# Moving a scan's chunk systems into the order in which the scan reads them: two ways of storing them

## The chip, the core and the metric

The kernel runs on one core of a Trainium2 chip, in one launch. The metric is the device time of one execution in microseconds; a lower number is better. The core has a matrix engine (TensorE, PE in the profile, with its weight loads listed as PEld), a vector engine (VectorE, DVE), a scalar engine (ScalarE, ACT), GpSimd (POOL) and SyncE (SP), which in this kernel only issues transfers. The sixteen DMA engines of the core carry out what SP's queue and ACT's queue issue.

## The reference, cut to what matters

The layer has an attention branch and a gated DeltaNet branch that scans the 256 context and 256 latent positions of 8 heads in both directions, in chunks of 64 positions. For each chunk the scan needs the solution of a unit lower triangular system of 64 by 64:

```python
m = jnp.where(strict, jnp.einsum('bhnid,bhnjd->bhnij', kb, k) * decay, 0.0)
rhs = jnp.concatenate([v * beta, kb * jnp.exp(gc)[..., None]], axis=-1)
sol = lax.linalg.triangular_solve(m + jnp.eye(c, dtype=m.dtype), rhs,
                                  left_side=True, lower=True, unit_diagonal=True)
u, w = sol[..., :dv], sol[..., dv:]
...
def step(s, inp):
    u_c, w_c, k_c, g_c = inp[:4]
    v_new = u_c - jnp.einsum('bhcd,bhde->bhce', w_c, s)
    s_next = s * g_c + jnp.einsum('bhcd,bhce->bhde', k_c, v_new)
```

There are 8 heads, 8 chunks and 2 directions, so 128 systems. The kernel does not solve them one by one: it inverts all 128 matrices at once and multiplies by the inverse inside the scan.

## The kernel before, in words

The program is a chain of stages. Weights are read in float32 in tiles of 128 by 1024 (`raw`, a ring of 8 buffers), split into a rounded part `whi` (ACT, L123) and a remainder `wlo` (DVE, L124), and multiplied with activations that are split in the same way. A second user of the ring are the tiles `rawa` of the modulation matrix, which DVE reduces beside all stages.

1. **First projection** (to about 145 us). The activations `xl` and `xc` arrive in eight transfers of 512 KB, their squares are summed on PE (`pss`), and for each of 16 slices of the model dimension the modulation columns (`wt`, `raw<-in_wadab`) and the first weights (`gr<-in_wfirst`) are used as soon as they land (`amp`, `fp`).
2. **The heads' stage** (to about 390 us). For each head, the rest of the input projection and `dn_head`, which among other things makes the strictly triangular matrix `U` of each chunk. `U` is stored to DRAM as blocks of 32 by 32: the two diagonal blocks to `Ud`, the off-diagonal one to `Uo`.
3. **The inverse** (`inverse`, L822, run in pieces beside the key and value projections, to about 480 us). All 128 systems lie on the 128 partitions of `ux`: partition 32 g + 16 d + s holds system (g, d, s), where d is the direction, g is a head modulo 4 and s counts chunk and half of the heads. DVE inverts both diagonal blocks. The result is stored twice: as `Xq` for the off-diagonal product (8 stores, L846), and into `Tt` by 16 stores (L851), one for each g, d and diagonal block b. Each of them moves 512 runs of 128 bytes.
4. **The latent attention** (to about 700 us). Beside the attention's matmuls and the gate projections (`gtp`), `off_diagonal` (L854) makes the off-diagonal blocks in 8 rounds q: it loads `uo` and `xd`, multiplies twice with block-diagonal matrices (`ivp`) and stores the product to `Tt` with 4 transfers a round (L892, 128 runs of 128 bytes each).
5. **The scan** (from about 720 us) reads `Tt`, one piece for each chunk (`tt<-Tt`, L1273). `Tt[64 d + 32 b + c, s, g, 32 e + j]` is row 32 b + c, column 32 e + j of the inverse. The block that is always zero (rows of b = 1, columns below 32) is stored once, from a tile of zeros, `none`, by two transfers of 2048 runs of 128 bytes (L656).
6. Branch projections, output projection and the gated feed-forward layer fill the rest.

What sets the order: PE's instructions are kept in the order in which the program is written (`pe.pinned`) for nearly all of it. The other engines and the two queues are ordered by a scheduler that places an instruction where it believes its inputs to be ready. `osync` is SP with its order kept. A generator such as `off_diagonal` runs as a `Side`: it is called with an allowance, and each `yield` says how much of it was used up.

Two rules of the built program matter below. The completion of a transfer is signalled on one of eight semaphores, `DMAHW0` to `DMAHW7`, which SP's and ACT's transfers share in rotation; a transfer that is given a semaphore waits until the transfer that had it before has landed. And a tile that is laid where another tile was waits for the last reader of the old one: the pool `pc2` of the attention, in which the small tile `km` of `k_norm` (L1035) lies, reuses the space of `ux`.

Of the kernel before, what the change touches and what calls it, by code (L numbers as in the profile page):

```python
# [8 lines left out]
F32 = mybir.dt.float32  # L9
# [44 lines left out]
def hybrid_block(ctx: ExitStack, tc: tile.TileContext, io, dbg=None):  # L54
    nc = tc.nc
    act, dve, pool, sync = nc.scalar, nc.vector, nc.gpsimd, nc.sync
# [19 lines left out]
    osync = Ordered(nc.sync)  # L76
# [3 lines left out]
    def pool_(name, bufs, side="left"):  # L80
        return tc.tile_pool(name=name, bufs=bufs, side=side, reuse_waits="tile")
# [8 lines left out]
    dram = ctx.enter_context(tc.tile_pool(name="dram", bufs=1, space=DRAM))  # L90
# [10 lines left out]
    none = const.tile([P, 32], F32, name="none")  # L101
# [154 lines left out]
    def ada_rest():  # L256


        def load(i):
            w = wr.tile([P, GR], F32, tag="raw", name="rawa", bufs=NR)  # L260
            c, n = divmod(i, 32)
            sync.dma_start(w, io["wada2"][c, (n // 16 + c) % 2, n % 16])
            return w

        parts = ad.tile([P, 2, 16], F32, name="parts")
        half, ahead = None, [load(0), load(1)]
        for i in range(128):
            c, n = divmod(i, 32)
            h, j = (n // 16 + c) % 2, n % 16
            if h != half:  # L270

                for _ in range(1 if i else 0):
                    yield 1300
                half, sch = h, ad.tile([P, GR], F32, tag="sch", name="sch")
                sync.dma_start(sch, Sc[h])
                for _ in range(3):
                    yield 1300
            w = ahead.pop(0)
            if i < 126:
                ahead.append(load(i + 2))  # L280
            (odve if ada.bound else dve).tensor_tensor_reduce(out=w, in0=w, in1=sch, scale=1.0, scalar=0.0, op0=ALU.mult, op1=ALU.add, accum_out=parts[:, h, j : j + 1])  # L281
            if n == 31:
                cs = slice(16 * c, 16 * c + 16)
                dve.tensor_tensor(out=adaT[:, cs], in0=parts[:, 0], in1=parts[:, 1], op=ALU.add)
                dve.tensor_tensor(out=adaT[:, cs], in0=adaT[:, cs], in1=bada[:, 32 + 16 * c : 48 + 16 * c], op=ALU.add)
                ada.done = c + 1
            yield 1300
# [240 lines left out]
    for j in range(2 * N1):  # L528
        dst = dkx[:, j].rearrange("p a b -> p (a b)")
# [59 lines left out]
    g = pg.tile([P, 8, 8], F32, name="gx")  # L589
# [60 lines left out]
    Ud = dram.tile([4, 32, 2, 32, 32], F32, name="Ud")  # L650
    Uo = dram.tile([4, 32, 32, 32], F32, name="Uo")

    Xq = dram.tile([2, 32, 4, 32, 32], F32, name="Xq")
    Tt = dram.tile([P, 16, 4, 64], F32, name="Tt")
    for d in range(2):
        act.dma_start(Tt[64 * d + 32 : 64 * d + 64, :, :, 0:32].rearrange("c s g j -> c (s g) j"), none[:32].unsqueeze(1).broadcast_to([32, 64, 32]))  # L656
    As = dram.tile([4, P, 8, 64], F32, name="As")
    conv = mid.tile([P, 24, 3], F32, name="conv")
    dve.tensor_scalar(out=conv, in0=off["dn_conv"].rearrange("p (f w) -> p f w", w=3), scalar1=0.5, scalar2=None, op0=ALU.mult)
# [114 lines left out]
    def head_inputs(h, side=lambda c: None):  # L774
# [12 lines left out]
        gather(ps, P, xq[:, 0])  # L787
        return xs[0], xs[1], xq

    ada = Side(ada_rest())  # L790
    ada.done, ada.bound = 0, True
    ins = {h: head_inputs(h) for h in (3, 0)}
# [29 lines left out]
    def inverse():  # L822


        pI = ExitStack()
        pi = pI.enter_context(pool_("pi", 1, "right"))
        ux = pi.tile([P, 2560], F32, name="ux")
        flat = ux[:, 0:2048]
        X = flat.rearrange("p (b c j) -> p b c j", b=2, j=32)
        tmp = ux[:, 2048:]  # L830
        sync.dma_start(flat, Ud.rearrange("g r b j i -> (g r) (b j i)"))
        yield 0
        for j in range(1, 31):
            m = 31 - j
            t = tmp[:, : 2 * j * m].rearrange("p (b c i) -> p b c i", b=2, i=m)
            dve.tensor_tensor(out=t, in0=X[:, :, 0:j, j].unsqueeze(3).broadcast_to([P, 2, j, m]),
                              in1=X[:, :, j, j + 1 :].unsqueeze(2).broadcast_to([P, 2, j, m]), op=ALU.mult)
            dve.tensor_tensor(out=X[:, :, 0:j, j + 1 :], in0=X[:, :, 0:j, j + 1 :], in1=t, op=ALU.add)
            yield 150 + 4.2 * j * m
        dve.memset(flat.rearrange("p (b x) -> p b x", b=2)[:, :, 0:1024:33], 1.0)  # L840
        xt = pi.tile([P, 32, 32], F32, name="xt")
        act.copy(xt, X[:, 0].rearrange("p c j -> p j c"))
        for g in range(4):
            gs = slice(32 * g, 32 * g + 32)
            for n, x in enumerate((xt, X[:, 1])):
                sync.dma_start(Xq[n, :, g], x[gs])  # L846
        for g in range(4):
            for d in range(2):
                for b in range(2):
                    rs = slice(64 * d + 32 * b, 64 * d + 32 * b + 32)  # L850
                    sync.dma_start(Tt[rs, :, g, 32 * b : 32 * b + 32].rearrange("c s j -> s c j"), X[32 * g + 16 * d : 32 * g + 16 * d + 16, b])  # L851
        yield 1000
        pI.close()

    def off_diagonal():

        pI = ExitStack()
        pi = pI.enter_context(pool_("pj", 1, "right"))
        bd = [pi.tile([P, 4, P], F32, name=f"bd{n}") for n in range(2)]
        for n in range(2):  # L860
            pool.memset(bd[n], 0.0)

        def load(q):
            rs = slice(4 * q, 4 * q + 4)
            uo = pi.tile([P, 4, 32], F32, tag="uo", name="uo", bufs=2)
            sync.dma_start(uo, Uo[:, :, rs].rearrange("g j r i -> (g j) r i"))
            xd = pi.tile([P, 2, 4, 32], F32, tag="xd", name="xd", bufs=2)
            for n in range(2):
                sync.dma_start(xd[:, n], Xq[n, rs].rearrange("r g j c -> (g j) r c"))
            return uo, xd  # L870

        ahead = load(0)
        yield OD
        for q in range(8):
            uo, xd = ahead
            if q < 7:
                ahead = load(q + 1)
            for n in range(2):
                src = uo if n == 0 else ip
                for g in range(4):  # L880
                    gs = slice(32 * g, 32 * g + 32)
                    act.copy(bd[n][gs, :, gs], src[gs])
                yield OC / 2
                ip = psa.tile([P, 4, 32], F32, tag="aux", name="ivp")
                for r in range(4):
                    pe.matmul(ip[:, r], bd[n][:, r], xd[:, n, r], start=True, stop=True)
                if n == 0:
                    yield OC / 2
            act.copy(uo, ip)
            for g in range(4):  # L890
                dst = Tt[64 * (q // 4) : 64 * (q // 4) + 32, 4 * (q % 4) : 4 * (q % 4) + 4, g, 32:64]
                sync.dma_start(dst, uo[32 * g : 32 * g + 32])  # L892
            yield OC / 2
        pI.close()

    Ys = dram.tile([P, HEADS, T], F32, name="Ys")
# [44 lines left out]
    pn = pN.enter_context(pool_("pn", 1))  # L941
    pn2 = pN.enter_context(pool_("pn2", 2))
    inv = Side(inverse())
    inv(1)
    bq = pn.tile([P, 1, T], F32, name="bq")
# [43 lines left out]
    pN.close()  # L989
    pc2 = pC.enter_context(pool_("pc2", 2))  # L990
    inv = Side(off_diagonal())

    def mm3(ps, a, b, first, last):
# [206 lines left out]
    for b in range(4):  # L1200
# [4 lines left out]
        for n in range(7):  # L1205
            for st in (pr, tail, at):
                c = next(st, None)
# [286 lines left out]
    for f in range(NFF):  # L1494
        xs = []
        for w in ("wgate", "wval"):
# [6 lines left out]
            x = pf2.tile([P, T], F32, tag=w, name="fx")  # L1503
# [13 lines left out]
    for f in range(KD):  # L1517
# [8 lines left out]
        src = ps[:, :T]  # L1526
        if f < KD - 1:
            gather(ps, P, yx)
            src = yx
# [105 lines left out]
```

## Time and profile before

| | |
|---|---|
| median of 3 runs | 1783.9 us (1779.87 to 1786.72) |
| the profiled execution | 1786.89 us, span of its instructions 1785.1 us |
| PE busy in the span | 1737.5 us (97%) |
| DVE, ACT, POOL busy | 1356.8, 950.5, 41.4 us |
| DMA | 190,260 packets, 417.15 MB, 56,912 packets under 512 bytes |
| matmul clock granted, mean | 0.985 of full speed |

The page's row of tenths cuts the span into 40 slices of 44.6 us; a digit is the busy share of an engine in that slice, 9 standing for 90% or more. `PEclk` is the granted matmul clock in tenths. In a view of windows, each row gives the busy time of an engine in a stretch, and at its end the granted clock, the share of the time in which the sixteen DMA engines were busy, and the GB/s that they moved. In a view of waits, a row reads: engine and line that waited, what ended the wait, total us, number of times, longest. In a timeline, a row starts with the time at which a run of equal instructions started and its length in us; SPq and ACTq are issues of transfers.

### The profile page before, as it was taken

To read this page: it belongs to the slowest core of one execution; us is meant where nothing else is said; L and a number is where in the kernel's file an instruction comes from. 1 tells how busy PE (TensorE), PEld (TensorE's weight loads), DVE (VectorE), ACT (ScalarE), POOL (GpSimd) and SP (SyncE) were. 2 spreads that over 40 slices of the span, in tenths; PEclk is the share of its full clock that TensorE was granted. 3 is DMA by queue.
4 is the path that set the end of the run, shared out by engine and by line. 5 is a ranking of instruction groups with operands and counts; after the bars stand their busy time and mean duration, and the time that the engine had idled before them with its cause. 6 is when DMAs were issued, how large, how long until landed. Compare 5 with 4: busy or idle time off the path is not lost.

```text
span 1785.1 us, 34155 instructions
## 1 busy us (share of the span) xinstructions
PE 1737.5 (97%) x12957; PEld 1507.2 (84%) x12957; DVE 1356.8 (76%) x2696; ACT 950.5 (53%) x1966; POOL 41.4 (2%) x48
## 2 busy tenths in 40 slices
PE   7999999999799999999999999999999999999999
PEld 5887888888688888788878888888888888888888
DVE  4677799879578879787779979887788887655554
ACT  3335454454477766665646546555555555544443
POOL 0000011000000000000010000000000000000000
PEclk8999999999899999999989999999999999999999
DMA  9992588783578868999647968776667776666662
GB/s 348 407 373 93 150 235 249 230 257 109 138 255 248 260 214 273 360 339 361 233 130 233 328 199 281 232 237 207 202 219 229 228 225 201 182 198 199 198 199 87
DMA packets 190260, 417.15 MB, mean 234 GB/s; under 512 B 56912, under 2 KB 95696, under 8 KB 187792
## 3 DMA queue, kind: packets, MB, share of 16 engines
q1 hardware_dynamic: 165024, 401.59, 68.7%
q10 hardware_dynamic: 25072, 13.39, 2.5%
q8 instruction: 101, 1.65, 0.4%
q14 instruction: 63, 0.52, 0.1%
HBM read 387.00 MB, written 27.79 MB: 232 GB/s over the span
## 4 chain that ended last, share of the span: by engine, by line
PE 63%; issue 8%; DMA 1%; DVE 1%; ACT 0%; SPq 0%; POOL 0%; POOLq 0%; DVEq 0%
PE fps L68 27%; PE dps L68 13%; PE gtp L68 11%; PE brp L68 3%; PE vps L68 1%; PE kps L68 1%; PE qps L68 1%; PE sps L68 1%; PE kp L68 1%; PE ivp L68 1%; PE op L68 1%; PE yps L68 1%; PE yp L68 0%; DMA YM<-Ys 0%; SPq L851 0%
## 5 line engine op out<-in xcount | busy, mean ns | idle before, releaser
L123 ACT CAST whi<-raw 128x512 fp32r<-128x512 f32 (+1 forms) x940 | 578.9, 620 | 413.6 <-PE dps L68 113.5
L124 DVE TENSOR_TENSOR wlo<-raw,whi 128x512 fp32r<-128x512 f32 (+1 forms) x940 | 637.3, 686 | 211.4 <-ACT whi L123 203.5
L68 PE MATMUL fps<-H,whi 128*128 128x512 f32 x1376 | 475.0, 394 | 3.1 <-DVE H L1472 3.1
L68 PE MATMUL fps<-H,wlo 128*128 128x256 f32 x1376 | 372.3, 280 | 0.0
L68 PEld LDWEIGHTS fps<-H,whi 128*128 128x128 f32 x1376 | 253.7, 189 | 54.7 <-issue 1.9
L68 PEld LDWEIGHTS fps<-H,wlo 128*128 128x128 f32 x1376 | 259.7, 189 | 7.5 <-DVE wlo L124 0.5
L68 PE MATMUL gtp<-h,whi 128*128 128x512 f32 x640 | 231.4, 399 | 0.0
L68 PE MATMUL mmp<-h,whi 128*128 128x512 f32 x640 | 229.5, 400 | 0.0
L68 PE MATMUL dps<-GB,whi 128*128 128x512 f32 (+1 forms) x595 | 195.7, 377 | 0.0
L68 PE MATMUL mmp<-h,wlo 128*128 128x256 f32 x640 | 177.5, 283 | 0.0
L68 PE MATMUL gtp<-h,wlo 128*128 128x256 f32 x640 | 173.9, 282 | 0.0
L68 PE MATMUL dps<-GB,wlo 128*128 128x256 f32 x560 | 155.2, 282 | 0.0
L68 PEld LDWEIGHTS gtp<-h,whi 128*128 128x128 f32 x640 | 120.5, 190 | 25.3 <-issue 0.9
L68 PEld LDWEIGHTS mmp<-h,whi 128*128 128x128 f32 x640 | 119.8, 189 | 24.9 <-ACT dkx L531 0.3
L68 PEld LDWEIGHTS dps<-GB,whi 128*128 128x128 f32 x595 | 109.2, 188 | 20.2
L68 PEld LDWEIGHTS gtp<-h,wlo 128*128 128x128 f32 x640 | 121.5, 190 | 4.5
L68 PEld LDWEIGHTS mmp<-h,wlo 128*128 128x128 f32 x640 | 121.8, 190 | 3.6 <-issue 1.4
L68 PEld LDWEIGHTS dps<-GB,wlo 128*128 128x128 f32 x560 | 105.8, 189 | 0.6
L281 DVE CUSTOM_DVE_ANT_0 rawa<-rawa,sch 128x1024 f32<-128x1024 f32 x68 | 82.9, 1222 | 20.9 <-DMA rawa<-in_wada 19.4
L68 PE MATMUL fp<-h,gh 128*128 128x256 f32 (+1 forms) x448 | 85.5, 291 | 2.5 <-ACT h L68 1.7
L68 PEld LDWEIGHTS fp<-h,gh 128*128 128x128 f32 (+1 forms) x448 | 69.7, 190 | 7.6 <-issue 4.1
L68 DVE CUSTOM_DVE_ANT_0 rawa<-rawa,sch 128x1024 f32<-128x1024 f32 x60 | 72.9, 1218 | 0.0
(574 smaller groups left out, 2563.4 us busy)
## 6 DMA issues: line engine op xcount, KB each, us to landing
rawa<-in_wada SPq DMA_DIRECT2D x128, 512.0 KB, 5.2
raw<-in_wgate SPq DMA_DIRECT2D x82, 512.0 KB, 4.4
raw<-in_wval SPq DMA_DIRECT2D x82, 512.0 KB, 4.6
raw<-in_wdown SPq DMA_DIRECT2D x80, 512.0 KB, 4.2
wt<-in_wadas SPq DMA_DIRECT2D x16, 1024.0 KB, 9.6
raw<-in_wadab SPq DMA_DIRECT2D x32, 512.0 KB, 11.6
raw<-in_wgm SPq DMA_DIRECT2D x32, 512.0 KB, 5.6
raw<-in_wgd SPq DMA_DIRECT2D x32, 512.0 KB, 6.9
```

Source lines behind the costliest of these rows:

```text
L68: i = f(*a, **k)
L123: act.copy(hi, raw)
L124: dve.tensor_tensor(out=lo, in0=raw, in1=hi, op=ALU.subtract)
L281: (odve if ada.bound else dve).tensor_tensor_reduce(out=w, in0=w, in1=sch, scale=1.0, scalar=0.0, op0=ALU.mult, op1=ALU.add, accum_out=par ...
```

## The change

Four edits belong together.

- The two stores of zeros into `Tt` leave ACT's queue at the start of the program and become two transfers on SP's queue, written just before the heads' stage.
- `inverse` no longer stores into `Tt`. It stores a third plane of `Xq` instead: the diagonal blocks of b = 0 untransposed, so 12 stores of 128 KB instead of 8.
- `off_diagonal` takes over the diagonal blocks. In each round q, two transfers from `Xq` (DRAM) to `Tt` (DRAM) put the two diagonal blocks of that round's 16 systems (one direction, four s, four g) in their place (`place`).
- The off-diagonal blocks no longer go from `uo` to `Tt` by 4 stores of 16 KB a round on SP. ACT stores them with one transfer of 64 KB to a new DRAM tensor `Xo`, and one round later SP moves them from `Xo` to `Tt`.

Every transfer between `Xq` or `Xo` and `Tt` moves 512 runs of 128 bytes. What is computed, and what `Tt` holds when the scan starts, is the same.

```diff
-    Xq = dram.tile([2, 32, 4, 32, 32], F32, name="Xq")
+    Xq = dram.tile([3, 32, 4, 32, 32], F32, name="Xq")
+    Xo = dram.tile([32, 4, 32, 32], F32, name="Xo")
     Tt = dram.tile([P, 16, 4, 64], F32, name="Tt")
-    for d in range(2):
-        act.dma_start(Tt[64 * d + 32 : 64 * d + 64, :, :, 0:32].rearrange("c s g j -> c (s g) j"), none[:32].unsqueeze(1).broadcast_to([32, 64, 32]))
...
+    for d in range(2):
+        osync.dma_start(Tt[64 * d + 32 : 64 * d + 64, :, :, 0:32].rearrange("c s g j -> c (s g) j"), none[:32].unsqueeze(1).broadcast_to([32, 64, 32]))
     ada = Side(ada_rest())
...
-            for n, x in enumerate((xt, X[:, 1])):
+            for n, x in enumerate((xt, X[:, 0], X[:, 1])):
                 sync.dma_start(Xq[n, :, g], x[gs])
-        for g in range(4):
-            for d in range(2):
-                for b in range(2):
-                    rs = slice(64 * d + 32 * b, 64 * d + 32 * b + 32)
-                    sync.dma_start(Tt[rs, :, g, 32 * b : 32 * b + 32].rearrange("c s j -> s c j"), X[32 * g + 16 * d : 32 * g + 16 * d + 16, b])
         yield 1000
...
-                sync.dma_start(xd[:, n], Xq[n, rs].rearrange("r g j c -> (g j) r c"))
+                sync.dma_start(xd[:, n], Xq[2 * n, rs].rearrange("r g j c -> (g j) r c"))
             return uo, xd
+
+        def place(q, b, c, src):
+            rows = slice(64 * (q // 4) + 32 * b, 64 * (q // 4) + 32 * b + 32)
+            dst = Tt[rows, 4 * (q % 4) : 4 * (q % 4) + 4, :, 32 * c : 32 * c + 32]
+            sync.dma_start(dst.rearrange("c s g j -> (s g) c j"), src[4 * q : 4 * q + 4].rearrange("s g c j -> (s g) c j"))
...
+            for n in range(2):
+                place(q, n, n, Xq[1 + n])
+            if q:
+                place(q - 1, 0, 1, Xo)
...
             act.copy(uo, ip)
-            for g in range(4):
-                dst = Tt[64 * (q // 4) : 64 * (q // 4) + 32, 4 * (q % 4) : 4 * (q % 4) + 4, g, 32:64]
-                sync.dma_start(dst, uo[32 * g : 32 * g + 32])
+            act.dma_start(Xo[4 * q : 4 * q + 4].rearrange("r g c i -> (g c) r i"), uo)
             yield OC / 2
+        place(7, 0, 1, Xo)
         pI.close()
```

How the built program moves is shown at three places. The first is the start of ACT's queue before: `cv` and `sel` are small inputs, `Tt<-none` are the zeros, `sq<-xl` the squares of the activations.

```order
L306 DMA cv<-in_cv 128x32
L321 DMA sel<-in_sel 128x3
L656 DMA Tt<-none 2048x1x32
L309 ACT_TABLE_LOAD
L309 ACTIVATE cth<-cv 128x32
L68 ACTIVATE sq<-xl 128x4x256 x2
L656 DMA Tt<-none 2048x1x32
L68 COPY scb<-scp 128x512
```

The same two transfers stand in the change on SP, between the masks and the weights of the heads' stage.

```order
 L109 DMA masks<-in_masks 128x640
 L262 DMA rawa<-in_wada 128x1024
+L68 DMA Tt<-none 2048x1x32 x2
 L129 DMA raw<-in_wdv 128x1024 x2
 L262 DMA rawa<-in_wada 128x1024
```

With the zeros go two uses of the shared semaphores: what moved is also the semaphore on which the fourth transfer of `xc` waits.

The second place is SP's queue at the end of the inverse. Before, `Xq` is stored, then come the 16 stores into `Tt`, then the loads `xd` of round 0 and 1, and only then the next weights (`raw<-in_wz`, `rawa`, `raw<-in_wqb`).

```order
L846 DMA Xq<-xt 32x1024
L846 DMA Xq<-ux 32x1024
L851 DMA Tt<-ux 16x32x32 x16
L869 DMA xd<-Xq 128x4x32 x4
L129 DMA raw<-in_wz 128x1024
L262 DMA rawa<-in_wada 128x1024
L129 DMA raw<-in_wqb 128x1024
```

In the change, two transfers into `Tt` are ahead of the next weights; the rest follow in pairs between the weight loads of the attention.

```order
L847 DMA Xq<-ux 32x1024 x2
L865 DMA xd<-Xq 128x4x32 x2
L871 DMA Tt<-Xq 16x32x32
L865 DMA xd<-Xq 128x4x32 x2
L871 DMA Tt<-Xq 16x32x32
L129 DMA raw<-in_wz 128x1024
L262 DMA rawa<-in_wada 128x1024
L129 DMA raw<-in_wqb 128x1024
L129 DMA raw<-in_wz 128x1024 x2
L871 DMA Tt<-Xq 16x32x32 x2
L262 DMA rawa<-in_wada 128x1024 x2
```

So 14 transfers of 64 KB fewer stand between the last store of `Xq` and the next weight tile.

The third place is DVE's first `km` of the attention, with what it waits for; before:

```order
L930 SCALAR_TENSOR_TENSOR zx<-zt,zx 128x256 [waits Activation_49]
L1035 SCALAR_TENSOR_TENSOR km<-ks,krm 128x4 [waits DMAHW4_49,DMAHW3_49,DMAHW5_49,DMAHW2_49,DMAHW6_49,DMAHW1_49,DMAHW7_49,DMAHW0_49,PE_49]
L124 TENSOR_TENSOR kt<-kps,kt 128x512 [waits Activation_49]
```

and in the change:

```order
L934 SCALAR_TENSOR_TENSOR zx<-zt,zx 128x256 [waits Activation_49]
L1039 SCALAR_TENSOR_TENSOR km<-ks,krm 128x4 [waits DMAHW4_49,DMAHW2_49,DMAHW5_49,DMAHW1_49,DMAHW6_49,DMAHW0_49,PE_49]
L124 TENSOR_TENSOR kt<-kps,kt 128x512 [waits Activation_49]
```

`km` still waits for everything that reads `ux`; what reads it last is now a store to `Xq` and no longer a store to `Tt`. PE's order is the same in both programs from the first to the last instruction.

## The prediction

> **What bounds the kernel now.** I read the page's rows of tenths first, then windows at the two places where PE is short, then waits, chain and timelines there.
>
> ```profile
> PE   7999999999799999999999999999999999999999
> PEclk8999999999899999999989999999999999999999
> ```
>
> PE is full except in slice 0 and slice 10 (446 to 491 us), which also have a lowered clock. The change touches both: its zeros were issued in slice 0, its 16 stores in slice 10. Elsewhere only what delays PE's fixed order counts. Slice 10, windows cut where the granted clock changed:
>
> ```profile
> 465.05:471.88 6.83, 4.64 (x56) 3.78 (x55) 2.14 (x4) 3.50 (x8) 0.00 (x0) 1.00 0.34 53
> 471.88:485.54 13.66, 7.15 (x61) 6.68 (x61) 2.97 (x8) 1.06 (x2) 2.01 (x2) 0.50 0.68 125
> ```
>
> PE works 7.15 of 13.66 us there, at half clock. Waits from 440 to 500 us:
>
> ```profile
> ACT whi L123 <- DMA raw<-in_wz: 12.8, 1, 12.8
> DVE km L1035 <- DMA xd<-Xq: 10.9, 1, 10.9
> PE ks L68 <- DVE km L1035: 6.5, 1, 6.5
> PE ks L68 <- ACT ksq L1024: 2.2, 1, 2.2
> ```
>
> In a row of waits stand what waited, what ended it, total, times and longest. The second `ks` waits 6.5 us for DVE, which stands at `km`. The row blames `xd`, but `km` reads no `xd`: it lies where `ux` was and waits for the readers of `ux`, the last of the 16 stores, landing as `xd` is issued. Why so late is shown by the timelines of SP (three rows) and ACT (one), and by two pieces of the chain:
>
> ```profile
> 456.61 0.79 SPq L846 DMA_DIRECT2D Xq<-xt  x2
> 460.33 17.87 SPq L851 DMA_DIRECT2D Tt<-ux  x16
> 480.88 0.45 SPq L129 DMA_DIRECT2D raw<-in_wz  x1
> 470.27 0.33 ACTq L910 DMA_DIRECT2D Zs<-zx  x1
> 470.27 1.87 DMA Zs<-zx
> 472.15 0.30 SPq L851
> ```
>
> The stores hold SP for 17.87 us. Part is their own landing, eight at a time; part is a hold until 472.15, when ACT's `Zs`, which had the semaphore next, has landed. Behind the stores stands `raw<-in_wz`, for which ACT waits 12.8 us.
>
> **Term 1, the inverse's end.** In the change `ux` is read by 12 stores of `Xq`. `Xq`'s stores go out every 0.4 to 0.5 us (two in 0.79) and land in some 3 us (the median of `Tt<-ux` below), so from 456.6 us on, when `xt` is ready, the last lands near 465 us, the four added ones included. `km`'s other input, `ks`, is there only at 471.7 us. So `km` no longer waits, and what is late next is the 2.2 us for `ksq`, which stays: ACT's order up to it is the same. PE around it, its timeline first, then the chain:
>
> ```profile
> 471.29 0.43 PE L68 MATMUL ks<-ones,ksq 128*32 128x1 f32 x32 [2.19 <-ACT ksq L1024]
> 481.52 2.86 PE vps L68 x12
> 489.14 2.88 PE vps L68 x24
> 484.37 4.76 PE gtp L68 x24
> 499.45 4.18 PE gtp L68 x24
> ```
>
> Twelve `vps` take 2.86 us at half clock, 24 take 2.88 at full. The stretch loses 6.5 us of idle time, 1.4 us twice in the two groups of 12 `vps`, and 0.6 us in the first `gtp`: 9.9 us. Not all of it comes back if the clock falls at the 2.2 us gap again. Two other drops show the shortest stay:
>
> ```profile
> 157.86:161.27 3.41, 3.41 (x11) 2.02 (x9) 2.83 (x6) 0.14 (x1) 0.00 (x0) 0.50 0.00 0
> 400.20:403.62 3.42, 3.42 (x11) 2.56 (x10) 3.42 (x12) 1.53 (x4) 0.00 (x0) 0.50 0.68 253
> ```
>
> A stay of 3.41 us costs 1.7 us, one of 6.83 us 3.4 us. So the gain is 8.2 us with the short stay, 6.5 with the long one, 9.9 with none. I take 8.2: the drop at 471.88 closed a window in which PE's longest gap was that 2.2 us, and the 6.5 us gap came only afterwards. The Trainium skill (TensorE: Matmul & The Clock Gate, "Part 1: The HAM clock gate") has the clock fall after at least one idle window of about 3.4 us. By that a gap of 2.2 us would not lower it, and this term would be 9.9; the row at 471.88 does not agree.
>
> Nothing takes the wait's place at once: SP still holds until 472.15 for `Zs` (the second `Tt<-Xq` has that semaphore), then issues `raw<-in_wz`, 8.4 us earlier than now, which keeps its distance to a PE that is 8.2 us earlier.
>
> **Term 2, the start.** In this order: SP's timeline, the landing of the two transfers from `none`, PE's timeline, windows, and the queue of ACT's transfers from 0 to 20 us (packets, MB, share of 16 engines):
>
> ```profile
> 5.57 0.33 SPq L68 DMA_DIRECT2D xl<-in_xT  x1
> 15.58 0.33 SPq L68 DMA_DIRECT2D xc<-in_ctxT  x1
> DMA to landing us min/median/max: 7.3/10.6/13.9
> 15.09 1.06 PE L68 MATMUL pss<-sq,ones 128*32 128x512 f32 x8 [0.51 <-DVE sq L68]
> 21.14 1.81 PE L68 MATMUL pss<-sq,ones 128*32 128x512 f32 x8 [3.90 <-DVE sq L68]
> 35.13 0.53 PE L68 MATMUL fp<-h,gh 128*96 128x256 f32 x1 [1.75 <-ACT h L68]
> 0.00:2.00 2.00, 0.00 (x0) 0.00 (x0) 0.78 (x3) 0.00 (x0) 1.33 (x10) 1.00 0.15 21
> 0.00:20.00 20.00, 11.80 (x80) 8.63 (x80) 8.02 (x18) 6.71 (x8) 1.33 (x10) 1.00 0.90 267
> 20.00:40.00 20.00, 14.84 (x171) 10.64 (x172) 7.03 (x13) 7.83 (x17) 1.02 (x1) 0.70 1.02 413
> q10 hardware_dynamic: 4416, 0.54, 17.9%
> ```
>
> The first store of zeros takes 13.9 us, and SP, which has nothing else to issue first, waits for its semaphore from 5.9 to 15.58 us before the last `xc`; PE then stands 3.9 us and continues at half clock. In the first 20 us the queue of the zeros (q10) moves 0.54 of 5.33 MB with 17.9% of the engines' time. Without it 4.8 MB are left; at the 413 GB/s of the next 20 us, after 2 idle us, these take 13.6 us instead of 20. All weights land 6.4 us earlier. PE can follow: its last `pss` can start up to 3.9 us earlier, at full clock it takes 1.06 instead of 1.81, and the short products behind it run at a clock that over the row of 20 to 40 us is 0.70. After 41.8 us PE is full and DMA has no slack to give back:
>
> ```profile
> 40.00:120.00 80.00, 79.17 (x901) 67.24 (x901) 56.02 (x83) 26.87 (x59) 0.00 (x0) 0.99 1.00 399
> 34.98:41.80 6.82, 6.12 (x27) 5.83 (x28) 6.79 (x11) 2.69 (x6) 0.00 (x0) 0.50 1.01 402
> ```
>
> Both limits move together, so I take 6.4. The lower bound is the idle time alone, 3.9; the upper one adds the half-clock window of the second row (3.4 us), should it not come back: 9.8.
>
> **What is added, and its cover.** The zeros fall into the heads' stage on SP:
>
> ```profile
> 154.22 0.33 SPq L262 DMA_DIRECT2D rawa<-in_wada  x1
> 175.35 3.85 SPq L129 DMA_DIRECT2D raw<-in_wdv  x2
> 160.00:165.00 5.00, 5.00 (x19) 2.54 (x17) 3.33 (x6) 3.23 (x6) 0.00 (x0) 0.87 0.00 0
> ```
>
> SP idles 20 us there and the DMA engines are empty; two issues (at the slowest pace quoted, 3.85 us for two) and 3.6 us of engine time (17.9% of 20 us) fit. Uncovered, they would cost those 3.6 us. In the attention:
>
> ```profile
> 490.00:650.00 160.00, 160.00 (x1214) 140.93 (x1214) 131.21 (x280) 113.56 (x270) 7.80 (x7) 1.00 0.80 257
> q1 hardware_dynamic: 4335, 0.54, 64.0%
> Tt<-ux SPq DMA_DIRECT2D x7, 64.0 KB, 2.9
> SPq L1154 <- DVE ryx L520: 10.7, 3, 6.3
> ```
>
> The middle rows are from 473 to 480 us: 4335 packets of 128 bytes took 64% of 16 engines for 7 us, 16.5 ns each. The attention gains 24 transfers of 512 and 8 of 512 (`Xo`), and loses 32 of 128: 12,288 packets more, 768 an engine, 12.7 us at that price, in 160 us of which the engines leave 20%, 32 us, free. A copy from DRAM to DRAM is not in the trace; its price lies between 13 ns (the zeros, 3.6 us over 276 packets an engine) and, if reading, writing and an answer follow one another, three times 16.5 (rival c). I take 16.5, which is nearest to its writing side, hence nothing on the path. ACT issues 8 transfers more, 0.33 us as for `Zs`, perhaps 0.45: ACT is busy 113.56 of 160 us and PE never waits there, so I take 0; uncovered it is 3.6 us. SP issues 24 transfers into `Tt` in place of 48, and DVE's and ACT's changed order moves only work that PE does not wait for in that row.
>
> **The sum.** 1786.89 (profiled) − 8.2 − 6.4 = 1772.3. That execution lies 3.0 above the median of 1783.9, so on the runs' scale I predict **1769**. For the ends: with 9.8 + 9.9 it is 1764, and 3 us of scatter make 1761; with 3.9 + 6.5 − 3.6 it is 1777, and 2 us make 1779.
>
> **Rivals.** (a) *The start is swallowed* (7%): DMA is at 1.00 and PE full from 40 to 120 us, so an early start could be lost to the next late weight; 1775.7. Against it: the weights themselves land earlier. (b) *The wait moves* (5%): `km` goes, but ACT's wait for `in_wz` behind SP's hold at 472.15 stalls PE as long; only the start remains, 1777.5. Against it: the distance above. (c) *The DMA engines become the bound* (4%). At 49.5 ns a packet, three times the row, the added packets need 38 us of 32 free: 6 us late, 1775.3. It decides from 42 ns. The Trainium skill (DMA: Bandwidth & Descriptors, "Specifications") says that below 512 bytes an engine reads, modifies and writes; the row of 16.5 ns is for such writes into DRAM and so contains that cost, only the read side from DRAM is new. (d) *Slower* (5%): SP is held behind `Xo`. `uo` of the next round and `Tt<-Xo` wait until ACT has issued `Xo` and it has landed, and behind them in SP's queue stand `raw` and `rawa`, for which ACT, and then PE, would wait. The hold from 460.33 to 480.88, 20.5 us, made ACT wait 12.8, so 7.7 us were covered. Eight rounds with a hold of 11 us would cost 8 × 3.3 = 26 us: 1796. It decides from 9.5 us (7.7 + 14.6 / 8). Against it: SP's longest wait from 490 to 650 us is 6.3 us, and PE was not short. (e) *It does not do what it says* (3%): the transfers bunch up again or the zeros collide; 1784. The forecast keeps 76%.
>
> **Chances.** A change of 0.5% (8.9 us, below which I call it the same) puts the border at 1775.0. Faster: nearly all of the 76% and some of (a) and (c), 0.79. Slower by more than that: (d), 0.05. The same: 0.16. The range of 1761 to 1779 leaves out (d), (e) and a little on both sides.
>
> **What would show it.** Right: no hold of SP at the last `xc`, first `fp` near 28.7 us instead of 35.13, DMA near 400 GB/s already from 2 us; `km` without a DMA wait, the second `ks` without 6.5 us; PE at 160 of 160 in the attention, with a DMA share near 0.87. Wrong: `fp` early but the stage still ending at 145 us (a); ACT's wait for `in_wz` with PE idle (b); packets above 42 ns (c); rows of PE or ACT waiting for weights, with SP waiting on `Xo` (d).

## The result, and the profile after

The changed kernel takes 1827.3 us (median of 4; 1820.5 to 1830.1), the kernel before beside it 1784.0: a ratio of 1.024, 95% interval 1.0205 to 1.0274. The forecast was 1769. The profiled execution took 1830.1 us, its span 1828.3.

The page of the changed kernel, PE's tenths and the granted clock:

```profile
PE   7999999999888799899999998999999999999999
PEclk9999999999899889999999999999999999999999
```

Slice 10, which the change was to fill, is somewhat better, and slices 11 to 13, which were full, are not. Where the time is won and lost is read from four landmarks of the program (the first product of the first stage, the first `ks`, the first `ivp`, the scan's first load) in the timelines, first of the changed kernel, then of the one before where its row was not shown yet:

```profile
29.86 0.53 PE L68 MATMUL fp<-h,gh 128*96 128x256 f32 x1 [1.75 <-ACT h L68]
465.20 0.43 PE L68 MATMUL ks<-ones,ksq 128*32 128x1 f32 x32 [2.19 <-ACT ksq L1028]
468.05 0.61 PE L68 MATMUL ks<-ones,ksq 128*32 128x1 f32 x32
480.55 0.97 PE L68 MATMUL ivp<-xd,bd 128*128 128x32 f32 x8
765.55 0.65 SPq L1277 DMA_DIRECT2D tt<-Tt  x1
```

```profile
494.64 0.97 PE L68 MATMUL ivp<-xd,bd 128*128 128x32 f32 x8
721.66 0.51 SPq L1273 DMA_DIRECT2D tt<-Tt  x1
```

The changed kernel is 5.3 us ahead at `fp` (35.13 before), 6.1 at `ks`, 14.1 at the first `ivp`: both terms of the forecast are there, 14.1 of 14.6 us. At the scan's first load it is 43.9 us behind, and at the end of the span 43.2. So 58 us are lost between the first `ivp` and the scan, 54 of them in the eight rounds (the last `ivp` starts at 670.7 us, 190.1 behind the first; before, at 630.9 us, 136.3 behind the first), and nothing is lost behind the scan's first load. Windows of the changed kernel there; before, PE was busy 160.00 of 160 us from 490 to 650:

```profile
480.00:500.00 20.00, 14.49 (x77) 12.32 (x76) 13.24 (x26) 10.28 (x27) 0.00 (x0) 0.83 0.54 166
600.00:620.00 20.00, 15.07 (x65) 12.42 (x64) 10.65 (x22) 9.95 (x23) 0.00 (x0) 0.74 0.55 197
480.00:660.00 180.00, 149.12 (x1007) 125.79 (x1006) 109.51 (x233) 95.43 (x229) 6.96 (x6) 0.91 0.58 182
```

No engine is full over this stretch: the share of the DMA engines, the bound of rival (c), is 0.58, where 480 to 660 us had 0.79 before. What SP waits for from 480 to 660 us, and one piece of the chain:

```profile
SPq L865 <- PE ivp L68: 48.8, 4, 14.4
SPq L865 <- PE ks L68: 14.8, 1, 14.8
SPq L871 <- DMA Xo<-uo: 10.9, 1, 10.9
SPq L129 <- DVE wlo L124: 9.0, 3, 3.9
SPq L862 <- DMA Xo<-uo: 5.7, 5, 1.9
```

```profile
594.63 2.11 DMA Xo<-uo
596.74 0.02 SPq L862
...
599.43 5.14 DMA raw<-in_wgm
604.57 0.02 issue
604.60 0.63 ACT whi L123
605.22 0.04 issue
605.27 3.23 PE gtp L68 x8
```

L865 is `xd<-Xq`, L862 `uo<-Uo`, L871 a transfer into `Tt`, L129 a weight load; `whi` is the weight's cast on ACT, `gtp` a gate projection on PE. SP stands for TensorE's work and for `Xo`, and a weight that stands behind is then on the path. That is the pattern of rival (d), in a size and at a transfer that it did not name. Whether it is the cause, the experiments have to show.

### The profile page after: what moved, and what is told of

Same layout as the page of the kernel before. It is cut to its first block, busy times and chain, and to the rows that moved or that the text cites. A ratio compares the mean times of both kernels' runs of the same rounds, so it can differ in the third digit from the quotient of the medians.

```text
span 1828.3 us, 34110 instructions
## 1 busy us (share of the span) xinstructions
PE 1756.0 (96%) x12957; PEld 1516.8 (83%) x12957; DVE 1359.0 (74%) x2696; ACT 949.0 (52%) x1966; POOL 41.6 (2%) x48
## 4 chain that ended last, share of the span: by engine, by line
PE 59%; issue 8%; DVE 3%; DMA 3%; ACT 1%; POOL 0%; SPq 0%; ACTq 0%; POOLq 0%; DVEq 0%
PE fps L68 26%; PE dps L68 13%; PE gtp L68 10%; PE brp L68 2%; DMA raw<-in_wgm 1%; PE vps L68 1%; PE kps L68 1%; DVE wlo L124 1%; PE ivp L68 1%; PE kp L68 1%; PE qps L68 1%; PE op L68 1%; DVE rawa L68 1%; PE sps L68 1%; ACT whi L123 0%
## 5 line engine op out<-in xcount | busy, mean ns | idle before, releaser
L68 PE MATMUL gtp<-h,whi 128*128 128x512 f32 x640 | 242.7, 414 | 22.3 <-ACT whi L123 22.3
L68 PE MATMUL gtp<-h,wlo 128*128 128x256 f32 x640 | 180.0, 291 | 1.8 <-DVE wlo L124 1.8
L68 PEld LDWEIGHTS gtp<-h,whi 128*128 128x128 f32 x640 | 125.7, 197 | 50.9 <-ACT whi L123 25.0
L68 PEld LDWEIGHTS gtp<-h,wlo 128*128 128x128 f32 x640 | 126.6, 198 | 9.9 <-DVE wlo L124 5.4
```

The costliest lines, as they stand in the source:

```text
L68: i = f(*a, **k)
```

## The experiments

The theories, as the expectations name them. **T1**: SP stands at transfers that wait for TensorE (`xd`; in a wider form also `uo`, `Tt<-Xo`, `Ys`), with weights behind. **T2**: the build gave ACT and DVE another order, in which casts of weights (`whi` on ACT, `wlo` on DVE) stand behind copies that wait for TensorE. **T3**: the transfers from DRAM to DRAM cost the time themselves. **T4**: SP is held by `Xo`. `bd` are the copies of `uo` and of the first product into the block-diagonal matrices, on ACT; `km` and `qm` are small tiles of the norms of keys and queries, on DVE and POOL, and `rb` is made of `km`; `Ys<-ryx` (L1158) stores the attention's result. TensorE's own order is the same, row for row, before and after. All times are medians; the kernel before had 1783 to 1786 beside them.

### One hold at a time: e1, e2, e5

```diff
-            xd = pi.tile([P, 2, 4, 32], F32, tag="xd", name="xd", bufs=2)
+            xd = pi.tile([P, 2, 4, 32], F32, tag="xd", name="xd", bufs=4)      # e1, e5
-            uo = pi.tile([P, 4, 32], F32, tag="uo", name="uo", bufs=2)
+            uo = pi.tile([P, 4, 32], F32, tag="uo", name="uo", bufs=4)         # e2, e5
-            if q:
-                place(q - 1, 0, 1, Xo)
+            if q > 1:
+                place(q - 2, 0, 1, Xo)                                         # e5
```

> The change with one edit: xd has 4 buffers instead of 2, so that the load xd<-Xq no longer has to wait until TensorE has read the buffer two rounds back. The order on ACT and DVE is the change's but for 4 or 5 rows, TensorE's is identical. T1 (SP stands at xd<-Xq, which waits for TensorE's ivp, with weights behind it in its queue; 63.6 us of such holds from 480 to 640 us): the waits of SP at L865 go, TensorE is full again from 500 to 650 us, and the loss of 1827 - 1769 us comes back: 1765 to 1775. T2 (ACT's changed order, casts behind copies that wait for TensorE): ACT's order stays, so 1820 to 1830. T3 (the DRAM to DRAM transfers themselves delay the weights): they stay, 1820 to 1830. T4 (SP is held behind Xo, by Tt<-Xo and uo): stays within 10 of 1827.

> The change with one edit: uo has 4 buffers instead of 2, so that the load uo<-Uo no longer waits for the landing of Xo<-uo two rounds back. T4 (SP held behind Xo): most of the loss comes back, 1770 to 1790. T1: the holds at xd stay, only the 5.7 us at uo go, 1817 to 1830. T2 and T3: no change, 1820 to 1832.

> The change with xd and uo in 4 buffers each and Tt<-Xo issued one round later, so that none of SP's transfers of the scan's order has to wait for work of TensorE of the same round. T1 in its wider form (SP stands at whichever of xd, uo or Tt<-Xo waits for TensorE, weights behind it): all such holds go, 1765 to 1775. T2 (the order built for ACT and DVE: the casts whi and wlo that TensorE needs next stand behind bd and zx copies, which wait for TensorE's previous product): 135 to 185 casts stand ahead of the 16 groups of bd copies, nearly as few as in the change, so 1810 to 1828.

Measured: 1822.4, 1828.2 and 1829.4 us. T1 in its first form and T4 fall. Two of SP's waits in e1, from 480 to 660 us:

```profile
SPq L862 <- DMA Xo<-uo: 49.0, 5, 12.7
SPq L1158 <- DVE ryx L520: 24.2, 3, 11.5
```

The hold only moved, from `xd` to the `uo` behind it, which waits for the landing of `Xo`, so for the same round of TensorE. In e5 SP waits neither for `xd` nor `uo`, but 39.0 us at `Ys<-ryx` and 18.4 us, at weight loads, for landings of `Xo` (480 to 700 us); that e5 would be free of holds was wrong, so it did not yet speak against the wide T1.

### The two terms by themselves: e3, e4, e9

```diff
 e3 (before):  the two stores of zeros from act.dma_start to osync.dma_start, ahead of the heads' stage
 e4 (e1):      the same two stores back on ACT at the start
 e9 (e3):
-                    sync.dma_start(Tt[rs, :, g, 32 * b : 32 * b + 32]...
+                    (sync if d else act).dma_start(Tt[rs, :, g, 32 * b : 32 * b + 32]...
```

> The kernel before with only the two stores of zeros moved from ACT's queue at the start to SP ahead of the heads' stage; the 16 stores and uo's 32 stay. If the start's gain is kept to the end: 1784 - 6.4 (as forecast) to 1784 - 8.8 (the lead of the changed kernel at 445 us), so 1775 to 1778. If it is swallowed later: 1782 to 1785.

> e1 with the zeros put back on ACT's queue at the start: what the change to the scan's order (three Xq, Xo, DRAM to DRAM) is worth without the start and without the hold at xd. T1 with the forecast's first term: 1784 - 8.2, so 1774 to 1778. If that term is smaller than forecast: 1778 to 1784. T2, T3, T4: 1828 to 1840.

> Before with the zeros moved (e3) and its 16 stores of Tt<-ux shared out: 8 issued by SP, 8 by ACT, no DRAM to DRAM transfer, no Xo. ACT's order is before's but for the issues (casts ahead of the groups of bd copies are the same numbers as before in all 16). T2 (loss from the order alone) with the forecast's two terms: km waits no more than 3 us, first ivp near 479 to 482 us, and PE full to 700 us: 1768 to 1775. If the stores on ACT hold up its casts instead: 1776 to 1784.

e3: 1779.9, ratio 0.997 (0.9958 to 0.9983): the start is worth 5.4 us; e4 against e1 gives 1829.3 − 1822.4 = 6.9. The forecast had 6.4. e9: 1778.6, ratio 0.9968 (0.9956 to 0.998). `km`'s wait went, but another took its place: ACT's own issue of its stores. ACT's timeline:

```profile
446.60 10.11 ACTq L851 DMA_DIRECT2D Tt<-ux  x6
456.75 0.42 ACT L929 ACTIVATE zt<-zx 128x256 f32<-128x256 f32 x1 [8.53 <-DMA Tt<-ux]
```

ACT, with TensorE's casts behind, stands until 456.75 us (TensorE waits 9.7 us for one of them), and the first `ivp` comes at 485.52, only 0.4 us ahead of e3's. The expectation of 479 to 482 was wrong.

### The transfers elsewhere: e6, e7, e8, e10, e11, e12

```diff
 e6:  place(q, n, n, Xq[1 + n])            issued by pool.dma_start
 e7:  place(q, n, n, Xq[1 + n])            left out; 4 more stores of zeros ahead of the heads' stage
 e8:  all 16 behind the eight rounds, at once
 e10: place(q, n, n, Xq[1 + n])            issued by act.dma_start
 e11: joined into 4 transfers of 2048 rows, in rounds 2, 3, 5, 6
 e12: all 16 behind the eight rounds, two by two
```

> The change with its 16 diagonal DRAM to DRAM transfers issued by POOL instead of SP; Tt<-Xo stays on SP. The transfers are the same, but ACT's order is built nearly as before the change: ahead of the fourth to eleventh group of bd copies stand 139, 141, 147, 147, 155, 157, 164, 164 casts (before 139, 141, 147, 148, 156, 157, 164, 164; the change 135, 135, 143, 143, 153, 157, 160, 160). T2: PE full from 500 to 650 us and 1768 to 1778. T3 (the transfers themselves, by their packets): 1815 to 1830. T1: xd, uo and Tt<-Xo still stand on SP and wait for TensorE, so 1800 to 1828.

> The change without its 16 diagonal transfers (in their place zeros are stored in the heads' stage, so the scan's diagonal blocks are zero: that part of the computation is left out). Its order on ACT is that of e6 in the groups of bd copies. T2: the transfers cost nothing on the chip, so within 5 of e6, 1765 to 1778. T3: 30 to 58 below e6 if that one is slow. T1: as e6.

> The change with its 16 diagonal transfers emitted on SP at the end of the rounds, not in them; Xo stays in the rounds. Casts ahead of the fourth to eleventh group of bd copies: 139, 140, 147, 147, 155, 157, 164, 164, nearly as before. T2: 1768 to 1780. T1 (holds at xd, uo and Xo remain on SP): 1800 to 1828. T3: the transfers come late in a row of 12, 1780 to 1830.

> The change with its 16 diagonal DRAM to DRAM transfers issued by ACT in the rounds instead of SP. Same transfers, same destination, same rounds as the change; casts ahead of the fourth to eleventh group of bd copies: 137, 141, 145, 149, 155, 157, 162, 166 (the change 135, 135, 143, 143, 153, 157, 160, 160; before 139, 141, 147, 148, 156, 157, 164, 164). T2: most of the loss is gone, 1768 to 1785. T3 (transfers spread over the rounds cost by themselves): 1815 to 1830.

> The change with its 16 diagonal transfers joined into 4 of 2048 rows, issued by SP in rounds 2, 3, 5 and 6; the same bytes and packets. Casts ahead of the fourth to eleventh group of bd copies: 139, 140, 147, 147, 153, 157, 164, 164. T2: 1768 to 1782. T3: the same packets, so 1815 to 1830.

> The change with its 16 diagonal DRAM to DRAM transfers left on SP and still issued two by two between weight loads, but behind the eight rounds (in the program's second half of the latent attention) instead of in them; Xo stays in the rounds. Casts ahead of the fourth to eleventh group of bd copies: 139, 140, 147, 147, 155, 157, 164, 164 (before 139, 141, 147, 148, 156, 157, 164, 164; the change 135, 135, 143, 143, 153, 157, 160, 160). T2 (the order of the casts): PE full from 480 to 600 us, and behind that no stall above 5 us: 1766 to 1778, of the forecast's size. T3 (the transfers, wherever they are spread): the loss moves to 600 to 700 us, 1800 to 1830. T1 (holds of SP for TensorE at xd and Xo, which remain): 1800 to 1828.

Measured: e6 1784.0, e7 1783.7, e8 1790.7, e10 1789.3, e11 1784.0, e12 1802.3. The same bytes and packets, issued elsewhere, cost 25 to 43 us less than in the change, and leaving them out saves no more than the best of these: T3 in its plain form falls. But none reached what T2 expected. In e6 POOL takes some 4 us for each of its transfers (0.6 us to issue, and 3.6 ahead of it, the mean of the second row below), and a power of the head norm (`qm`), for which DVE waits, stands behind:

```profile
DVE qm L1116 <- POOL qm L175: 9.2, 1, 9.2
POOL Tt L871 <- issue: 32.3, 9, 6.0
```

In e7 TensorE stands 8.8 us once, for a cast between 200 and 240 us, far from the rounds; from 480 to 660 us it is busy 179.02 of 180. In e8 the transfers bunched up again on SP, and `raw<-in_wkvb`, for which ACT waits 13.7 us, came behind them:

```profile
624.49 8.09 SPq L871 DMA_DIRECT2D Tt<-Xq  x12
```

e12 was full until 580 us and lost its time where its transfers now were, from 640 to 740 us. The expectation of T2 was wrong there, and T3's came true, in place and size. Whether the transfers or the order is the cause in e12 no run tells apart, but the order had moved there too: the expectation had counted casts in the rounds alone, and in the built order of e12 `qm` of the last head stands behind 216 casts `wlo`, before the change behind 220. And SP has another wait, from 600 to 720 us:

```profile
SPq L129 <- DMA Gs<-zx: 24.0, 3, 10.6
```

A weight load there waits for the landing of a store of ACT with which it shares no data. Before the change a store of SP waited in the same way for ACT's `Zs`, with which it shared the semaphore.

Why e10 and e11 miss what T2 expected is open in part: in e10 TensorE is busy 169.62 of 180 us from 480 to 660 us, in e11 it is short in two of the eight windows of 20 us from 480 to 640 us.

### The order by itself: e13 to e17

These kernels use edges of order: an instruction is issued behind a given other one on its own queue, with no wait added (shortened here; `NoSync` marks such an edge).

```diff
+    for b in BD[4 * m : 4 * m + 4]:                       # bd copies of group m, on ACT (e13, e15)
+        tc.add_manual_dep(b.ins, CAST[k - 1].ins.name, NoSync)
+    tc.add_manual_dep(i.ins, RAW[n - 33].ins.name, NoSync)  # xd, uo, Tt<-Xo, Ys on SP behind n weight loads (e14, e15, e17)
+    tc.add_manual_dep(RAW[n - 32].ins, i.ins.name, NoSync)  # e16, on the kernel before: weight loads behind them
+    tc.add_manual_dep(i.ins, C[k - 1].ins.name, NoSync)     # e17: each operation on ACT and DVE behind k casts, as before
```

In e14 further edges keep ACT's casts behind the `bd` copies as in the change. What the edges put back, counted in the built order (weight loads ahead of the pairs of `xd` on SP; casts ahead of the fourth to eleventh group of `bd` on ACT; casts ahead of the first six `qm` on DVE):

| | SP | ACT | DVE | us |
|---|---|---|---|---|
| before | 102, 106, 110, 115, 118, 122 | 139, 141, 147, 148, 156, 157, 164, 164 | 139, 139, 164, 164, 193, 193 | 1784 |
| the change | 98, 103, 107, 113, 116, 120 | 135, 135, 143, 143, 153, 157, 160, 160 | 135, 135, 162, 162, 191, 191 | 1827 |
| e13 | as the change | `bd` nearly as before | as the change | 1821.3 |
| e14 | as before | as the change | 135, 135, 164, 164, 191, 191 | 1823.6 |
| e15 | as before | `bd` nearly as before | 137, 137, 162, 162, 191, 191 | 1824.9 |
| e16 (no transfers) | as the change | 137, 137, 143, 143, 153, 153, 160, 162 | 137, 137, 162, 162, 191, 191 | 1826.0 |
| e17 | as before | 139, 141, 147, 149, 156, 157, 164, 166 | as before | 1782.9 |

> The change with ACT's order alone put back: edges of order (no waits) keep each group of bd copies behind as many casts whi as it stood behind before the change (139, 141, 147, 149, 153, 156, 164, 164 for the fourth to eleventh group; the change 135, 135, 143, 143, 153, 157, 160, 160). SP's order is the change's, row for row. T2 (order of the casts): PE full from 480 to 660 us, 1768 to 1785. T1 in its wide form (SP's order: xd, uo, Tt<-Xo and Ys, which wait for TensorE, stand 2 to 4 weight loads earlier): 1815 to 1835. T3 (the transfers): 1815 to 1830.

> The change with SP's order alone put back: edges of order keep xd, uo, Tt<-Xo and Ys behind as many weight loads as before the change (the pairs of xd behind 102, 106, 110, 115, 118, 122 loads, the change 98, 103, 107, 113, 116, 120), and the casts stay behind the bd copies as in the change (135, 135, 143, 143, 153, 157, 160, 160). The DRAM to DRAM transfers stay where they are. T1 in its wide form (SP's order): PE full from 480 to 660 us, 1766 to 1780. T2: 1810 to 1830. T3: 1815 to 1830.

> The change with both orders put back by edges (e13 and e14 together); the transfers and their place on SP are the change's. T1 and T2 alike: 1764 to 1776, the forecast. T3 (the transfers themselves): 1815 to 1830.

> The kernel before with the zeros moved (e3, 1780), without any DRAM to DRAM transfer, but with SP's order of the change forced by edges: xd, Tt<-uo, uo and Ys stand 2 to 5 weight loads earlier (pairs of xd behind 98, 103, 107, 113, 116, 120 loads). The build then orders ACT's casts nearly as in the change too (137, 137, 143, 143, 153, 153, 160, 162). T1 and T2: 1815 to 1835, as slow as the change with none of its transfers. T3: 1780 as e3.

> The change with the order of all three queues put back by edges of order (no waits): on SP as in e14, on ACT and DVE every operation of the attention that writes something other than whi or wlo stays behind as many casts as before the change (bd: 139, 141, 147, 149, 156, 157, 164, 166 for the fourth to eleventh group; qm on DVE: 139, 139, 164, 164, 193, 193; the change 135, 135, 162, 162, 191, 191). e15 had put back only SP and the bd copies on ACT and was still slow; DVE's order was the change's there. All 24 transfers from DRAM to DRAM and the 8 of Xo stay where the change has them. If the loss is the order of the three queues (T2, wide): PE full from 480 to 700 us, and the forecast, 1766 to 1777. If it is the transfers (T3), or landings that SP waits for behind ACT's stores: 1810 to 1830.

e16 is the plainest: the kernel before, without one transfer from DRAM to DRAM, loses 46 us against e3 (1826.0 against 1779.9) when only the order is moved, on SP to the change's and on ACT and DVE nearly to it. The window in e3, then in e16:

```profile
480.00:660.00 180.00, 180.00 (x1405) 159.07 (x1404) 144.80 (x313) 126.00 (x297) 10.13 (x9) 1.00 0.76 244
480.00:660.00 180.00, 154.92 (x1055) 132.63 (x1055) 116.28 (x245) 100.77 (x242) 7.75 (x6) 0.91 0.55 184
```

e13, e14 and e15 came out as T3 had it: neither SP's order nor the casts against `bd`, nor both, bring the time back. But e16, which has none of the transfers and is slow, and e17, which has all of them and is not, rule T3 out. What T1 and T2 both missed is that one queue is not enough. In e15 no cast waits for a weight any more from 480 to 660 us; TensorE waits for the casts, for `whi` on ACT as for `wlo` on DVE (three of its rows), and the chain, from 528 to 533 us, runs through DVE:

```profile
PE gtp L68 <- ACT whi L127: 6.9, 5, 2.9
PE qps L68 <- DVE wlo L128: 5.2, 3, 2.9
PE qps L68 <- ACT whi L127: 5.2, 2, 2.8
```

```profile
528.24 0.42 PE ks L68 x32
...
528.68 0.16 DVE km L1046
...
528.98 1.93 POOL km L180
...
531.22 0.69 DVE rb_d L1020
531.90 0.61 DVE wlo L128
532.51 0.04 issue
532.56 1.44 PE vps L68 x5
```

`wlo` stands behind `km` and the three `rb`, which wait for TensorE's `ks`, and TensorE waits for `wlo`. On ACT, e15 put back the `bd` copies alone; the other operations that wait for TensorE still stand ahead of casts there. The lead of the weights was lost on three queues at once, and putting back one, or SP's with the `bd` copies, brings at most 6 us (e13 to e15). With all three back (e17) the kernel takes 1782.9, 44 us less than the change, with every one of its transfers in place.

That each of the three counts by itself is not shown: no run puts DVE's order, or all of ACT's, back alone. e10 speaks against so simple a rule: counted in its trace, its `qm` stand behind 136, 136, 162, 162, 191, 191 casts, nearly as in the change, its pairs of `xd` behind 101, 105, 109, 113, 118, 122 weight loads, nearly as before, and it takes 1789.3, 5 us more than the kernel before.

### The last 14 us: e18

e17 was still 14 us above the forecast. SP's waits of e17 from 470 to 610 us, then three rows of SP's timeline, and the landings of the two weights for which TensorE stood (line numbers are those of e17's kernel: L885 is `uo`, L888 `xd`, L894 the transfers into `Tt`):

```profile
SPq L885 <- DMA Xo<-uo: 24.4, 5, 6.6
SPq L888 <- PE ivp L89: 12.2, 5, 6.0
```

```profile
497.85 0.33 SPq L885 DMA_DIRECT2D uo<-Uo  x1
498.23 0.52 SPq L894 DMA_DIRECT2D Tt<-Xo  x1
498.81 1.29 SPq L894 DMA_DIRECT2D Tt<-Xq  x2
...
502.57 7.95 DMA raw<-in_wz
...
577.50 7.10 DMA raw<-in_wgm
```

Each late weight was issued in the burst behind a hold at `uo`, with three transfers from DRAM to DRAM among it, and took 7 to 8 us to land. e18 is e17 with the three edits of e5.

> e17 (all three orders put back) with xd and uo in 4 buffers each and Tt<-Xo issued one round later. In e17 SP still stood 24.4 us at uo<-Uo for the landing of Xo and 14.7 us at xd for TensorE between 470 and 610 us, and TensorE stood twice, at 510 and 585 us (7.2 us idle, 3.4 us of lowered clock), each time for weights issued behind such a hold. If these holds cause it (rival d of the forecast, in its real size): SP waits for neither uo nor xd, TensorE is full from 480 to 700 us, and the time is 10 us below e17's 1783: 1768 to 1776. If the two stalls come from the transfers themselves (the weights issued among them landed in 7 to 8 us instead of 4.5): 1779 to 1786.

Measured: 1773.8 us, ratio 0.9926 (0.9909 to 0.9942), faster than both kernels. Its window and its first load of the scan:

```profile
480.00:660.00 180.00, 179.36 (x1387) 157.85 (x1387) 144.10 (x315) 123.65 (x295) 11.17 (x9) 1.00 0.79 247
```

```profile
707.23 0.43 SPq L1314 DMA_DIRECT2D tt<-Tt  x1
```

SP no longer waits at `uo`, TensorE is full, and the transfers are the change's: at the scan the kernel is 721.66 − 707.23 = 14.4 us ahead of the one before, where the forecast had 14.6. By the medians it gains 12.0 of the 14.9 us that the forecast had on the runs' scale; where the other 3 are, no run shows. The holds that e5 took away in vain are worth 9 us once the order is right.

## Why the prediction was wrong, step by step

- **Term 1** (8.2 us): right in mechanism and size. `km`'s wait is gone, the 2.19 us for `ksq` stay, SP is held for `Zs` until 466.08 us, and ACT's wait for `in_wz` falls from 12.8 to 1.0 us, so rival (b) did not come. From the first `ks` to the first `ivp` TensorE takes 15.35 us instead of 23.35, 8.0 less. In e7, whose clock stays at 1.00 there, it takes 13.72, 9.6 less than before, where the forecast had 9.9 without a drop.
- **Term 2** (6.4 us): right in mechanism, a little too large. SP issues its last `xc` at 5.58 us, the first `fp` comes at 29.86 and not 28.7, and by itself the edit is worth 5.4 us (e3). It is not swallowed: rival (a) did not come.
- **The zeros' cover and the transfers' own price** (0): right. e18 carries all 32 and leads by 14.4 us at the scan. From 490 to 650 us its DMA share is 0.80, as before, and not 0.87, so the packets may cost less than the 16.5 ns taken, if that can be read from a share at all.
- **The step that failed** is the last of "What is added, and its cover": that SP's 24 transfers in place of 48 are free, and that "DVE's and ACT's changed order moves only work that PE does not wait for in that row". In the order before, the casts and weight loads stood far enough ahead of every operation that waits for TensorE, so that no wait showed in the row of 490 to 650 us. The row proves that the old order hides its waits; it was used as if it held for any order. The new one keeps, where the table counts, up to 6 fewer casts on ACT, 2 to 4 fewer on DVE and 2 to 4 fewer weight loads on SP ahead, and 44 us of the 58 come from that (e17); the order alone, without the transfers, costs 46 (e16). Another 9 are the holds at `uo`, `xd` and `Xo` (e17 to e18), which had been put at nothing with it.
- **Rival (d)** had the right kind of place, SP held with weights behind it, and 5%. Its price of 26 us by holds of 11 us at `Xo` is, with the order put right, 9 us (e17 to e18). What decided was not that hold alone but the lead that the order left to cover it: in e11, whose order is nearer to the old one, SP is held up to 10.9 us at `xd`, and TensorE is full in six of the eight windows of 20 us from 480 to 640 us.
- The range ended at 1779 and gave the side on which it came out 5%. The built order was at hand, in which the pairs of `xd` stand 2 to 4 weight loads earlier on SP; that was not priced.

What stays open: why the build moved the three orders (leaving the 16 transfers out, or issuing them from POOL, leaves them nearly as before; its reasons are in no trace), which queue, and which single operation of ACT or DVE, costs most, and why e10 is fast with DVE's counts nearly those of the change. In e16 ACT's and DVE's order followed SP's, so it shows the price of the three together, not of SP's.

## What to carry to other kernels

When a change adds transfers to a queue whose order a build sets, count for each queue how many weight loads and casts stand ahead of every operation that waits for TensorE, before and after; a loss of up to six places was worth 44 us here, and a trace of the old order shows none of it. Put an order right on all queues of the chain (load, cast, residual cast) at once: here a part of it put back brought at most 6 us, the whole 44. Free a wait (more buffers, a transfer a round later) and restore the order together: alone either gave nothing or part, both gave 53 us.

## What the runs showed of the hardware that was not expected

- A weight load on SP can wait for the landing of a store that ACT issues and that it shares no data with (24.0 us at `Gs<-zx` in e12; before the change a store of SP waited so for `Zs`, until 472.15 us): the built program gives the two the same semaphore in turn.
- POOL took some 4 us for each issue of 64 KB from DRAM to DRAM (e6, the rows above), SP 0.7 us (8.09 us for twelve, e8).
- The clock falls or stays at the same gaps. From 436 to 490 us the changed kernel and e7 are busy alike, with the same five gaps between products (0.7, 0.9, 1.1, 0.6 to 0.7 and 2.19 us); the first has a mean clock of 0.91, the second 1.00:

```profile
436.00:490.00 54.00, 48.58 (x375) 40.98 (x374) 35.39 (x77) 29.40 (x64) 3.13 (x3) 0.91 0.47 135
```

```profile
436.00:490.00 54.00, 48.54 (x457) 41.04 (x456) 41.40 (x88) 31.33 (x65) 4.12 (x5) 1.00 0.59 172
```

So the forecast's reading, that the gap of 2.2 us had lowered the clock, does not hold as a rule. The Trainium skill (TensorE: Matmul & The Clock Gate, "Part 1: The HAM clock gate") has the clock fall after at least one idle window of about 3.4 us: e7's row agrees with it; the changed kernel's, whose longest gap is 2.19 us, does not.
